# A decoder block on one core: transposes, products and casts placed by hand between the output and the up projection, and a ninth warm-up matmul

## The chip, the cores and the metric

The kernel runs on one core of one Trainium2 chip. The metric is the device time of one execution in microseconds (us), given as the median of several runs. Engines are named as the profile names them: PE (TensorE matmuls), PEld (its weight loads), DVE (VectorE), ACT (ScalarE), POOL (GpSimd), SP (SyncE, here only a DMA queue).

## The reference

One layer, 512 tokens, width 1024, all in float32: attention and pooling are merged through gates, then comes the output projection, an MLP with a squared ReLU, and a last norm.

```python
h = rmsnorm(x, norm_attn_g[l])
u = h @ w_in[l]
u_q, u_k, u_v, u_pool, u_gate = jnp.split(u, splits, axis=-1)
...
a = diff_attention(q, k, v, positions, lam, subln_g[l], lam_init)
p = multiscale_pool(u_pool, w_pool[l], pool_scale[l])
gates = jax.nn.sigmoid(u_gate.reshape(B, S, N_BRANCHES, D_MODEL))
merged = gates[:, :, 0] * a + gates[:, :, 1] * p
x = x + (merged @ w_out[l]).astype(x.dtype)
h2 = rmsnorm(x, norm_mlp_g[l])
z = jnp.square(jax.nn.relu(h2 @ w_up[l]))
x = x + (z @ w_down[l]).astype(x.dtype)
...
return rmsnorm(x, final_norm_g)
```

`w_out` is 1024x1024, `w_up` 1024x4096, `w_down` 4096x1024.

## The kernel before

Every float32 product is made of three matmuls in a rounded format: each operand is split into a high part (`wh`, `hi`, a cast on ACT) and a remainder (`wl`, `lo`, a subtraction on DVE), and high by high, remainder by high and high by remainder are summed in PSUM. So each block of weights costs a DMA, a cast and a remainder before PE may use it. Before the first real matmul stand warm-up matmuls on a tile of ones (`warm`).

The change lies in the passage from the output projection to the MLP.

- The output projection runs over two halves n of its 1024 columns, with `w_out` in blocks of two k-tiles (`wr_o`, `wh_o`, `wl_o`). For n=0 four banks (`po`, one for each group of 128 tokens, t=0 to 3) grow together. For n=1 each t has a bank of its own (`po` rows 0 to 3, 24 matmuls each, through `mm_rows`). `x1_add` adds a bank to the residual `x1` (DVE) and squares the sum (ACT, `square`), from which `row_scale` makes the norm's factor; `h2` (`h` in the profile) is the normed row (DVE).
- Eight transposes on PE for each t turn `h2` into two banks (`h2T`, b=0 and 1). t=0 and t=2 share two banks, t=1 and t=3 another two. From the banks come the operands of the MLP: `gab` (high part on ACT, remainder on DVE), plain copies `h2f` (t=0, 1) and `hw` (t=2, 3) on ACT, and from these by sums and differences the forms S1 to S4 in `gss` (`forms_h2`).
- The MLP runs in four quarters q of its 4096 inner columns. In each, `up(q)` makes seven products A11, A12, A22, S1, S2, S3, S4 of 2x2 blocks in place of eight (a Strassen-like scheme) and `down(q)` seven more. One up product is 48 matmuls of 256 columns in two halves i, each in its own bank (`um_0`, `um_1`); one down product is 24 matmuls of 512 columns (`dm`). For q=0 the order of the up products is A11, A12, S1, S2, S3, A22, S4.
- S2, S3 and A22 add onto the banks of A11. After each, the bank is read: `keep` copies it to `rawz` (ACT), `join` adds it to `rawz` (DVE), `z_of` applies ReLU and square (ACT). The next product may add onto a half only when that half was read.
- The weights of S1, S2 and A22 are sums that stand in one pair of buffers (`wga`): when DVE has read one form, a DMA with addition on POOL's queue makes the next. Those of A11, A12, S4 come by SP (`wr_u`), those of S3 are `wal`. For the down weights of A11 and S1, DVE makes the sum `wga_d` of `wr_d` and `wal_d`.

A planner sets the order on each engine from its own estimate of times; every engine then runs its list strictly in that order and waits on semaphores. `after(later, earlier)` gives the planner a rule of order between two instructions. Two of the existing ones are touched by the change, one in `up(q)` and one at its end:

```python
if q == 0 and form == A11 and i + p == 2 and k == 0:
    after(m, state["h2T"])
```

The first down product, A11 of `down(0)`, needs `z` of A11 and its weights, and no later up product; nothing but the planner holds it.

Of the kernel before, what the change touches and what calls it, by code (L numbers as in the profile page):

```python
# [21 lines left out]
NK = D // P  # L22
# [29 lines left out]
def block_kernel(ctx, tc, xT, x_tok, gains, pos, consts, w_in, w_v, w_pool, w_out, w_up, w_dn, out):  # L52
# [113 lines left out]
        compare_op=ALU.is_ge, fill=NEG, base=0, channel_multiplier=1,  # L166
    )
    warm = bank(7, "warm")
    for _ in range(8):
        T.matmul(warm[:, :P], lhsT=ones, rhs=ones, start=True, stop=True)  # L170


# [386 lines left out]

    def square(t, n, junk):  # L560

        A.activation(out=junk, in_=x1[:, t, n * 512 : n * 512 + 512], func=AF.Square, accum_out=st[:, t, n : n + 1])

    def row_early(t, n):

# [13 lines left out]
    def mm_rows(a_, t, k, w, start, stop):  # L579
        hi, lo = w  # L580
        sl, tsl = slice((k % 2) * 512, (k % 2) * 512 + 512), slice(t * P, t * P + P)
        T.matmul(a_, lhsT=mh[:, k, tsl], rhs=hi[:, sl], start=start, stop=False)
        T.matmul(a_, lhsT=mh[:, k, tsl], rhs=lo[:, sl], start=False, stop=False)
        T.matmul(a_, lhsT=ml[:, k, tsl], rhs=hi[:, sl], start=False, stop=stop)

    def x1_add(t, n, a_):
        xs = x1[:, t, n * 512 : n * 512 + 512]
        V.tensor_tensor(out=xs, in0=a_, in1=xs, op=ALU.add)
        square(t, n, R[t][:, 0:2, :].rearrange("p a t -> p (a t)"))

    def forms_h2(forms, x):

# [18 lines left out]
                mm_rows(po[t], t, k, w, k == 0, k == NK - 1)  # L611
    for t in range(NT):
        nc.sync.dma_start(out=x1[:, t, :], in_=x_tok[t])
    for t in range(NT):
        x1_add(t, 0, po[t])
        row_early(t, 0)
    g2b, _ = gain(R[4].rearrange("p b c -> p (b c)"), 0)
    ws = [get_w(w_out[1, kk], f"o1_{kk}", V) for kk in range(4)]
    for t in range(NT):
        a_ = bank(4 + t, f"po1_{t}")  # L620
        for k in range(NK):
            mm_rows(a_, t, k, ws[k // 2], k == 0, k == NK - 1)
        x1_add(t, 1, a_)
        V.scalar_tensor_tensor(out=h2[:, t % 2], in0=x1[:, t, :], scalar=row_scale(t, 1), in1=g2b, op0=ALU.mult, op1=ALU.mult)
        pv = []
        for b in range(2):
            pt = bank((t % 2) * 2 + b, f"h2T{t}_{b}")
            for j in range(4):
                k = 4 * b + j
                state["h2T"] = T.transpose(out=pt[:, j * P : j * P + P], in_=h2[:, t % 2, k * P : k * P + P], identity=ident)  # L630
            pv.append(pt.rearrange("p (j q) -> p j q", q=P))
        sl = slice((t % 2) * P, (t % 2) * P + P)
        if t > 1:

            A.copy(out=hw[:, 1, :, sl], in_=pv[0])
            V.tensor_tensor(out=hw[:, 0, :, sl], in0=pv[1], in1=hw[:, 1, :, sl], op=ALU.subtract)
            forms_h2((S1, S2), sl)
        if t == 3:
            forms_h2((S3,), slice(0, HS))
        for b in range(t // 2, 2):  # L640
            hi, lo = (gab[b][:, t // 2, i, :, sl] for i in range(2))
            A.copy(out=hi, in_=pv[b])
            part = V.tensor_tensor(out=lo, in0=pv[b], in1=f(hi), op=ALU.subtract)
            if t == 3:
                after(part, state[S3])
            if t < 2:
                A.copy(out=h2f[:, b, :, sl], in_=pv[b])
# [8 lines left out]
    def weights(src, q, nm, order):  # L656

        def raw(b, tag="wr", pool=wp):
            if b == 2:
                both = big.tile([P, 2, 1024], F32, tag="s1b", name=f"wr21_{nm}{q}")  # L660
                tiles = [both[:, c] for c in range(2)]
            else:
                tiles = [pool.tile([P, 1024], F32, tag=tag, name=f"{tag}_{nm}{b}_{q}_{c}", bufs=2) for c in range(2)]
            if b is not None:
                for c in range(2):
                    nc.sync.dma_start(out=tiles[c], in_=src[q, b, c])
            return tiles

        def plus(tiles, b):

            return [G.dma_start(out=tiles[c], in_=src[q, b, c], accum_op=ALU.add) for c in range(2)]  # L671

        def parts(rs, b, hold=None, add=None):

            third = nparts[0] % 3 == 2
            nparts[0] += 1
            out_ = []
            for c in range(2):
                hi, lo = (
                    (bk if third else wp).tile([P, 1024], F32R, tag=t_ + "b" * third, name=f"{t_}_{nm}{b}_{q}_{c}", bufs=2 if third else 4)  # L680
                    for t_ in ("wh", "wl")
                )
                if add is None:
                    cast = split_w(rs[c], hi, lo, eng=V)
                else:

                    cast = A.copy(out=hi, in_=rs[c])
                    A.mul(out=lo, in_=f(hi), mul=-1.0)
                    G.dma_start(out=lo, in_=src[q, add, c], accum_op=ALU.add)
                if hold:  # L690
                    after(cast, hold)
                out_.append((hi, lo))
            return out_

        early = nm == "u" and q == 0
        r11, al, ga = raw(0), raw(1, "wal", bk), raw(None, "wga", bk)
        for c in range(2):
            if early:
                nc.sync.dma_start(out=ga[c], in_=src[q, 0, c])
            else:  # L700
                V.tensor_tensor(out=ga[c], in0=r11[c], in1=al[c], op=ALU.add)
        if early:
            plus(ga, 1)
            plus(al, 3)
        for n, form in enumerate(order):
            if form == A11:
                yield parts(r11, "b11", zhi[q, S1] if nm == "d" and q else None)
            elif form == A12:
                yield parts(raw(2), "b21", zhi[q, A11] if nm == "d" and q else None)
            elif form == S4:  # L710
                yield parts(raw(3), "b22", None, 3 if nm == "d" and q == 3 else None)
            elif form == S3:
                yield parts(al, "t3", first[-1])
            else:
                w = parts(ga, f"t{form}", state["rows"] if form == S1 and early else None if form == S1 else first[-1])
                if form != A22:
                    adds = plus(ga, {S1: 3, S2: 2}[form])
                if form == S1 and not early:

                    for i in plus(al, 3):  # L720
                        after(i, adds[1])
                yield w
# [23 lines left out]
    def up(q):  # L746
# [3 lines left out]
        def product(form, name, onto=None):  # L750
            w, pa = next(W), onto or [acc(f"u{name}{q}_{i}") for i in range(2)]
            rh, rl = gf[form]
            first.append(None)
            for i in range(2):
                hi, lo = w[i]
                for p in range(2):
                    a_ = pa[i][:, p * HS : p * HS + HS]
                    for k in range(4):
                        c = slice((p * 4 + k) * P, (p * 4 + k) * P + P)
                        m = T.matmul(a_, lhsT=hi[:, c], rhs=rh[:, k, :], start=p + k == 0 and onto is None, stop=False, skip_group_check=True)  # L760
                        first[-1] = first[-1] or m
                        T.matmul(a_, lhsT=hi[:, c], rhs=rl[:, k, :], start=False, stop=False, skip_group_check=True)  # L762
                    for k in range(4):
                        c = slice((p * 4 + k) * P, (p * 4 + k) * P + P)
                        m = T.matmul(a_, lhsT=lo[:, c], rhs=rh[:, k, :], start=False, stop=k == 3, skip_group_check=True)  # L765
                        if q == 0 and form == A11 and i + p == 2 and k == 0:
                            after(m, state["h2T"])

            if form == A22:
                state["m4"] = m  # L770
            elif form == S4:
                after(first[-1], state["m4"])
            return pa

        def keep(pa, r):
            for a_, r_ in zip(bank_view(pa), halves(r)):
                A.copy(out=r_, in_=a_)  # L777

        def join(pa, r):
            for a_, r_ in zip(bank_view(pa), halves(r)):  # L780
                V.tensor_tensor(out=r_, in0=a_, in1=r_, op=ALU.add)

        def z_of(r, sign, pa=None):
            for i, r_ in enumerate(halves(r)):
# [7 lines left out]
            forms_h2((S4,), slice(0, HS))  # L792

        def first_block():
            join(product(A12, "m2"), R[0])
            z_of(R[0], 1.0)
            if q > 0:
                zsplit(q, A11, R[0])
# [30 lines left out]
    def down(q):  # L829
# [15 lines left out]
        def product(form, name, onto=None):  # L845
            w, pa = next(W), onto or [acc(f"d{name}{q}_{a}") for a in range(2)]
            first.append(None)
            for a in range(2):
                m, _ = mms(pa[a], form, w, a, (0, 512), onto is None or onto is m2 and q == 0)
                first[-1] = first[-1] or m  # L850
            return pa

        def to_x1(pa, r, n):
# [140 lines left out]
```

## Time and profile before

| | |
|---|---|
| median of three runs | 677.72 us (676.64 to 678.88) |
| profiled execution | 675.88 us, span 674.1 us |
| mean granted PE clock over the span | 0.997 |
| output projection, n=1 row 3, to the first up matmul | 341 to 348.9 us |
| up products of q=0 | 348.9 to 394.9 us |
| costliest lines of PE | the three matmuls of `down`, L839, L841, L842: 7 to 8% of the chain each; the three of `up`, L760, L762, L765: 7% each |

Times within the execution are counted from the start of the span. The other 1.78 us of the execution lie around the span. A row of a timeline gives start, length, engine, line, operation, tile written and tiles read, shape, how many equal instructions it merges, and in brackets the idle time of the engine before it with what ended it. A matmul's length is modelled, so the distance from start to start tells its cost.

### The profile page before, as it was taken

Reading aid. Unit: us, or ns where it says so; the run is one execution under the profiler, and the core shown is the slowest. Engines: PE = TensorE matmul, PEld = TensorE weight load, DVE = VectorE, ACT = ScalarE, POOL = GpSimd, SP = SyncE. Lnnn points to the kernel's source line nnn. Section 1 sums busy time; section 2 is a strip of 40 time slices with the busy share of each in tenths; the row PEclk is TensorE's granted clock in tenths of the full one; section 3 lists DMA queues with packets and bytes.
Section 4 is the critical chain, followed back from the end, with each engine's and each line's share of the span. In section 5 each row is a group of like instructions: output and inputs, shape, how many; then the busy total and the mean of one; then the engine's idle time right before and its main releaser. Section 6 shows DMA issues by size and latency. Waiting matters only on the chain.

```text
span 674.1 us, 9988 instructions
## 1 busy us (share of the span) xinstructions
PE 664.5 (99%) x3686; PEld 579.4 (86%) x3686; DVE 526.4 (78%) x882; ACT 461.9 (69%) x741; POOL 112.0 (17%) x130
## 2 busy tenths in 40 slices
PE   9999999999999999999999999999999999999995
PEld 7888888888888888888889988899889998899884
DVE  5955977799979986965478989657994599747995
ACT  7465577978887698883477976367743696356974
POOL 2001110142133212520202020202103021210120
PEclk9999999999999999999999999999999999999998
DMA  8516464435254364574964688775959579494863
GB/s 304 174 60 182 124 150 127 101 95 124 94 133 122 98 159 95 128 197 172 314 186 84 198 176 231 159 204 138 237 187 192 194 155 261 123 215 129 215 125 124
DMA packets 32880, 109.34 MB, mean 162 GB/s; under 512 B 4032, under 2 KB 4928, under 8 KB 32832
## 3 DMA queue, kind: packets, MB, share of 16 engines
q0 software_dynamic: 10656, 38.80, 32.1%
q1 hardware_dynamic: 21744, 69.38, 28.8%
q8 instruction: 29, 0.48, 0.3%
q10 hardware_dynamic: 432, 0.52, 0.2%
q14 instruction: 19, 0.16, 0.1%
HBM read 106.59 MB, written 2.10 MB: 161 GB/s over the span
## 4 chain that ended last, share of the span: by engine, by line
PE 89%; DMA 5%; issue 3%; ACT 2%; DVE 1%; SPq 0%; POOLq 0%
PE dm L839 8%; PE dm L841 7%; PE dm L842 7%; PE um L760 7%; PE um L765 7%; PE um L762 7%; DMA wga_uNone<-w_up 4%; PE v L235 2%; PE o L418 2%; PE ga L132 2%; PE ga L131 2%; PE k L132 2%; PE gp L135 2%; PE gp L132 2%; PE k L131 2%
## 5 line engine op out<-in xcount | busy, mean ns | idle before, releaser
L841 PE MATMUL dm<-wh_dt,z 128*128 128x512 f32 (+1 forms) x128 | 49.5, 387 | 0.0
L842 PE MATMUL dm<-wl_dt,z 128*128 128x512 f32 (+1 forms) x128 | 49.4, 386 | 0.0
L839 PE MATMUL dm<-wh_dt,z 128*128 128x512 f32 (+1 forms) x128 | 49.0, 387 | 0.0
L760 PE MATMUL um<-gss,wh_ut 128*128 128x256 f32 x192 | 48.1, 284 | 0.1
L762 PE MATMUL um<-gss,wh_ut 128*128 128x256 f32 x192 | 48.1, 283 | 0.0
L401 ACT ACTIVATE p<-p,st 128x128 f32<-128x128 f32 (+3 forms) x64 | 35.7, 558 | 14.1 <-DVE st L397 13.8
L857 DVE TENSOR_TENSOR x<-x,dm 128x512 f32<-128x512 f32 x48 | 32.6, 683 | 15.2 <-PE dm L842 15.0
L112 ACT CAST wh_ut<-wga_uNone 128x1024 fp32r<-128x1024 f32 x24 | 24.9, 1052 | 27.5 <-PE dm L841 19.5
L671 POOL DMA_DIRECT2D wga_dNone<-w_dn x16 | 14.2, 885 | 150.9 <-DVE wl_dt L113 150.9
L112 ACT CAST wh_ub<-wr_u 128x1024 fp32r<-128x1024 f32 x24 | 25.1, 1048 | 20.0 <-PE um L762 11.0
L113 DVE TENSOR_TENSOR wl_ut<-wga_uNone,wh_ut 128x1024 fp32r<-128x1024 f32 x24 | 29.0, 1223 | 11.4 <-ACT wh_ut L112 10.2
L842 PE MATMUL dm<-wl_db,z 128*128 128x512 f32 x96 | 37.2, 389 | 0.0
L841 PE MATMUL dm<-wh_db,z 128*128 128x512 f32 x96 | 37.2, 389 | 0.0
L760 PEld LDWEIGHTS um<-gss,wh_ut 128*128 128x128 f32 x192 | 36.8, 192 | 0.3 <-ACT rawz L777 0.3
L762 PEld LDWEIGHTS um<-gss,wh_ut 128*128 128x128 f32 x192 | 36.9, 192 | 0.0
L839 PE MATMUL dm<-wh_db,z 128*128 128x512 f32 x96 | 35.8, 390 | 0.0
L671 POOL DMA_DIRECT2D wga_uNone<-w_up x18 | 15.6, 865 | 121.6 <-DVE wl_ut L113 87.5
L113 DVE TENSOR_TENSOR wl_ub<-wr_u,wh_ub 128x1024 fp32r<-128x1024 f32 x24 | 29.1, 1220 | 8.1 <-ACT wh_ub L112 8.1
L112 ACT CAST wh_dt<-wga_dNone 128x1024 fp32r<-128x1024 f32 x24 | 24.9, 1049 | 14.6 <-issue 5.0
L736 DVE TENSOR_TENSOR z<-rawz,z 128x1024 fp32r<-128x1024 f32 x28 | 33.7, 1221 | 0.5 <-ACT z L733 0.5
L397 DVE CUSTOM_DVE_ANT_0 p<-s,mask 128x128 f32<-128x128 f32 (+3 forms) x64 | 30.3, 484 | 3.6 <-PE s L396 3.5
L113 DVE TENSOR_TENSOR wl_dt<-wga_dNone,wh_dt 128x1024 fp32r<-128x1024 f32 x24 | 29.1, 1221 | 4.5 <-ACT wh_dt L112 4.5
(324 smaller groups left out, 2206.4 us busy)
## 6 DMA issues: line engine op xcount, KB each, us to landing
wr_u<-w_up SPq DMA_DIRECT2D x24, 512.0 KB, 5.3
wr_d<-w_dn SPq DMA_DIRECT2D x24, 512.0 KB, 4.0
wga_uNone<-w_up POOLq DMA_DIRECT2D x18, 512.0 KB, 6.8
wga_dNone<-w_dn POOLq DMA_DIRECT2D x16, 512.0 KB, 5.5
wr_k<-w_in SPq DMA_DIRECT2D x8, 512.0 KB, 3.3
wr_ga<-w_in SPq DMA_DIRECT2D x8, 512.0 KB, 3.3
wr_gp<-w_in SPq DMA_DIRECT2D x8, 512.0 KB, 3.8
wl_ga<-w_in POOLq DMA_DIRECT2D x8, 512.0 KB, 5.5
```

The costliest lines, as they stand in the source:

```text
L112: ins = A.copy(out=hi[:, sl], in_=raw[:, sl])
L113: (eng or G).tensor_tensor(out=lo[:, sl], in0=raw[:, sl], in1=f(hi)[:, sl], op=ALU.subtract)
L132: T.matmul(acc, lhsT=hi[:, c], rhs=rl[k], start=False, stop=False)
L401: A.activation(out=pr[:, c, :N], in_=pr[:, c, :N], func=AF.Exp, scale=-1.0, bias=st[:, c : c + 1], accum_out=st[:, 2 + c : 3 + c])
L736: V.tensor_tensor(out=z[:, 1], in0=r, in1=f(z[:, 0]), op=ALU.subtract)
L760: m = T.matmul(a_, lhsT=hi[:, c], rhs=rh[:, k, :], start=p + k == 0 and onto is None, stop=False, skip_group_check=True)
L762: T.matmul(a_, lhsT=hi[:, c], rhs=rl[:, k, :], start=False, stop=False, skip_group_check=True)
L765: m = T.matmul(a_, lhsT=lo[:, c], rhs=rh[:, k, :], start=False, stop=k == 3, skip_group_check=True)
L839: m = T.matmul(a_, lhsT=zh, rhs=hi[:, sl], start=p == 0 and start, stop=False, skip_group_check=True)
L841: T.matmul(a_, lhsT=zl, rhs=hi[:, sl], start=False, stop=False, skip_group_check=True)
L842: end = T.matmul(a_, lhsT=zh, rhs=lo[:, sl], start=False, stop=p == 3, skip_group_check=True)
L857: V.tensor_tensor(out=xs, in0=xs, in1=pa[a], op=(ALU.add, ALU.subtract)[n])
```

## The change

No arithmetic changes and no byte more is moved, but for one more warm-up matmul. The rest is rules of order: the transposes of t=0 and t=1 come inside `po` row 3, those of t=2 and t=3 inside A11 and A12; the matmuls of the up products of q=0 follow each other half by half (`state["um"]`); the first down product follows the last up product; the cast of the last `w_out` block precedes the first squares; A12's joins follow the remainder of S2's form; and the casts of A22's weights follow the copy of S2 (`state["keep"]`).

```diff
-    for _ in range(8):
+    for _ in range(9):
         T.matmul(warm[:, :P], lhsT=ones, rhs=ones, start=True, stop=True)
...
+    sq0 = []
     for t in range(NT):
-        x1_add(t, 0, po[t])
+        sq0.append(x1_add(t, 0, po[t]))
         row_early(t, 0)
     g2b, _ = gain(R[4].rearrange("p b c -> p (b c)"), 0)
-    ws = [get_w(w_out[1, kk], f"o1_{kk}", V) for kk in range(4)]
+    ws = []
+    for kk in range(4):
+        raw, hi, lo = load_w(w_out[1, kk], f"o1_{kk}")
+        cast = split_w(raw, hi, lo, eng=V)
+        ws.append((hi, lo))
+    for ins in sq0:
+        after(ins, cast)
     for t in range(NT):
         a_ = bank(4 + t, f"po1_{t}")
         for k in range(NK):
-            mm_rows(a_, t, k, ws[k // 2], k == 0, k == NK - 1)
+            m, end = mm_rows(a_, t, k, ws[k // 2], k == 0, k == NK - 1)
+            if t > 1 and k == 0:
+                after(m, state["po"])
+        if 0 < t < 3:
+            for b in range(2):
+                after(state["h2T", t - 1, b], end)
+        state["po"] = end
...
+                if j == 1:
+                    state["h2T", t, b] = state["h2T"]
                 state["h2T"] = T.transpose(out=pt[:, j * P : j * P + P], in_=h2[:, t % 2, k * P : k * P + P], identity=ident)
...
+                if early and b == f"t{A22}":
+                    after(cast, state["keep"])
...
-                        if q == 0 and form == A11 and i + p == 2 and k == 0:
+                        if q == 0 and form == A12 and (i, p, k) == (1, 0, 0):
                             after(m, state["h2T"])
+                    if q == 0:
+                        if (form, i, p) == (A11, 0, 1):
+                            for b in range(2):
+                                after(state["h2T", 2, b], m)
+                        elif (form, i, p) == (A11, 1, 1):
+                            for b in range(2):
+                                after(state["h2T", 3, b], m)
+                        if form != A11 or i + p:
+                            after(begin, state["um"])
+                        state["um"] = m
...
-            join(product(A12, "m2"), R[0])
+            join(product(A12, "m2"), R[0], None if q else state[S2])
...
+            if q == 0 and form == A11:
+                after(first[-1], state["um"])
```

How the rules move instructions, at the places of which the prediction speaks.

PE, from the end of `po` row 3 to the first up matmuls, before (`h2T_0`, `h2T_1` are the two banks of one t; the first two groups of eight are t=0 and t=1, the last group begins t=2):

```order
L630 MATMUL h2T_0_3200<-ident,h_2987 128x128 [waits DVE_49]
L630 MATMUL h2T_0_3200<-ident,h_2987 128x128 x3
L630 MATMUL h2T_1_3205<-ident,h_2987 128x128 x4
L630 MATMUL h2T_0_3249<-ident,h_2987 128x128 [waits DVE_49]
L630 MATMUL h2T_0_3249<-ident,h_2987 128x128 x3
L630 MATMUL h2T_1_3254<-ident,h_2987 128x128 x4
L583 MATMUL po_3_3317<-wl_o_3_3164,vh 128x512
L584 MATMUL po_3_3317<-wh_o_3_3163,vl 128x512
L760 MATMUL um_0_3398<-gab_2989,wh_ub_0_0_3390 128x256 [waits Activation_49]
L760 MATMUL um_1_3399<-gab_2989,wh_ub_0_1_3394 128x256
L760 MATMUL um_0_3464<-gab_2990,wh_ub_0_0_3456 128x256 [waits Activation_49]
L630 MATMUL h2T_0_3298<-ident,h_2987 128x128 [waits Activation_49]
```

The same place now, from the middle of `po` row 3:

```order
L645 MATMUL h2T_0_3201<-ident,h_2988 128x128 [waits DVE_49]
L645 MATMUL h2T_0_3201<-ident,h_2988 128x128 x3
L645 MATMUL h2T_1_3206<-ident,h_2988 128x128 x4
L582 MATMUL po_3_3318<-wh_o_2_3158,vh 128x512
L583 MATMUL po_3_3318<-wl_o_2_3159,vh 128x512
L584 MATMUL po_3_3318<-wh_o_2_3158,vl 128x512
L582 MATMUL po_3_3318<-wh_o_2_3158,vh 128x512
L583 MATMUL po_3_3318<-wl_o_2_3159,vh 128x512
L645 MATMUL h2T_0_3250<-ident,h_2988 128x128 [waits DVE_49]
L645 MATMUL h2T_0_3250<-ident,h_2988 128x128 x3
L645 MATMUL h2T_1_3255<-ident,h_2988 128x128 x4
L584 MATMUL po_3_3318<-wh_o_2_3158,vl 128x512
```

t=0's transposes moved from behind the 22nd matmul of row 3 to behind its 12th, t=1's to behind its 17th. The transposes of t=2, which began behind three up matmuls, now stand near the end of A11:

```order
L778 MATMUL um_1_3400<-gab_2990,wh_ub_0_1_3395 128x256
L781 MATMUL um_1_3400<-gab_2990,wh_ub_0_1_3395 128x256
L645 MATMUL h2T_0_3299<-ident,h_2988 128x128 [waits DVE_49,PE_49,Activation_49]
L645 MATMUL h2T_0_3299<-ident,h_2988 128x128 x3
L645 MATMUL h2T_1_3304<-ident,h_2988 128x128 [waits PE_49,Activation_49]
L645 MATMUL h2T_1_3304<-ident,h_2988 128x128 x3
L784 MATMUL um_1_3400<-gab_2990,wl_ub_0_1_3396 128x256 x4
L778 MATMUL um_0_3465<-gab_2991,wh_ub_0_0_3457 128x256
```

All eight of t=2 stand in one piece ahead of A11's last four matmuls, and A12 (`um_0_3465`) follows.

ACT, around the copies of S2 out of its banks (`COPY rawz<-um_0_3398` and `um_1_3399`; the `wh_ub` casts are weights of S4, the `wh_ut` casts those of A22, `gss` is the S4 form), before:

```order
L777 COPY rawz<-um_1_3531 128x512 [waits PE_49]
L112 CAST wh_ub_0_0_3775<-wr_u_0_0_3771 128x1024 [waits DMAHW7_49,PE_49]
L777 COPY rawz<-um_0_3398 128x512 [waits PE_49]
L112 CAST wh_ut_0_0_3704<-wga_uNone_0_3382 128x1024 [waits DMASW4_49]
L112 CAST wh_ut_0_1_3708<-wga_uNone_1_3383 128x1024 [waits DMASW5_49]
L112 CAST wh_ub_0_1_3779<-wr_u_0_1_3772 128x1024 [waits DMAHW0_49,DVE_49,PE_49]
L603 CAST gss_2992<-hw 128x1024 [waits DVE_49]
L777 COPY rawz<-um_1_3399 128x512 [waits PE_49]
```

and now (`um_0_3399` and `um_1_3400` are the same banks):

```order
L112 CAST wh_ub_0_0_3776<-wr_u_0_0_3772 128x1024 [waits DMAHW7_49,PE_49]
L817 ACTIVATE rawz<-rawz 128x512 [waits Activation_49]
L806 COPY rawz<-um_0_3399 128x512 [waits PE_49]
L112 CAST wh_ub_0_1_3780<-wr_u_0_1_3773 128x1024 [waits DMAHW0_49,PE_49]
L806 COPY rawz<-um_1_3400 128x512 [waits PE_49]
L603 CAST gss_2993<-hw 128x1024 [waits DVE_49]
L112 CAST wh_ut_0_0_3705<-wga_uNone_0_3383 128x1024 [waits DMASW4_49]
L112 CAST wh_ut_0_1_3709<-wga_uNone_1_3384 128x1024 [waits DMASW5_49]
```

The copy of S2's second half moved ahead of the S4 form and of both casts of A22's weights.

DVE, around the joins of S3 (`rawz<-um`, first and second half), from the remainder of S4's first weights, before:

```order
L113 TENSOR_TENSOR wl_ub_0_0_3776<-wr_u_0_0_3771,wh_ub_0_0_3775 128x1024 [waits DMAHW7_49,PE_49,Activation_49]
L113 TENSOR_TENSOR wl_ut_0_0_3705<-wga_uNone_0_3382,wh_ut_0_0_3704 128x1024 [waits DMASW4_49,Activation_49]
L113 TENSOR_TENSOR wl_ut_0_1_3709<-wga_uNone_1_3383,wh_ut_0_1_3708 128x1024 [waits DMASW5_49,Activation_49]
L113 TENSOR_TENSOR wl_ub_0_1_3780<-wr_u_0_1_3772,wh_ub_0_1_3779 128x1024 [waits DMAHW0_49,PE_49,Activation_49]
L781 TENSOR_TENSOR rawz<-um_0_3398,rawz 128x512 [waits PE_49]
L604 TENSOR_TENSOR gss_2992<-hw,gss_2992 128x1024 [waits Activation_49]
L701 TENSOR_TENSOR wga_dNone_0_3863<-wr_d_0_0_3855,wal_d_0_0_3859 128x1024 [waits DMAHW5_49,DMAHW3_49,DVE_49]
L736 TENSOR_TENSOR z_0_3760<-rawz,z_0_3760 128x1024 [waits Activation_49]
L113 TENSOR_TENSOR wl_db_0_0_3868<-wr_d_0_0_3855,wh_db_0_0_3867 128x1024 [waits Activation_49]
L781 TENSOR_TENSOR rawz<-um_1_3399,rawz 128x512 [waits PE_49]
```

and now:

```order
L113 TENSOR_TENSOR wl_ub_0_0_3777<-wr_u_0_0_3772,wh_ub_0_0_3776 128x1024 [waits DMAHW7_49,PE_49,Activation_49]
L113 TENSOR_TENSOR wl_ub_0_1_3781<-wr_u_0_1_3773,wh_ub_0_1_3780 128x1024 [waits DMAHW0_49,PE_49,Activation_49]
L604 TENSOR_TENSOR gss_2993<-hw,gss_2993 128x1024 [waits Activation_49]
L810 TENSOR_TENSOR rawz<-um_0_3399,rawz 128x512 [waits PE_49]
L113 TENSOR_TENSOR wl_ut_0_0_3706<-wga_uNone_0_3383,wh_ut_0_0_3705 128x1024 [waits DMASW4_49,Activation_49]
L113 TENSOR_TENSOR wl_ut_0_1_3710<-wga_uNone_1_3384,wh_ut_0_1_3709 128x1024 [waits DMASW5_49,Activation_49]
L753 TENSOR_TENSOR z_0_3761<-rawz,z_0_3761 128x1024 [waits Activation_49]
L718 TENSOR_TENSOR wga_dNone_0_3864<-wr_d_0_0_3856,wal_d_0_0_3860 128x1024 [waits DMAHW5_49,DMAHW3_49,DVE_49]
L810 TENSOR_TENSOR rawz<-um_1_3400,rawz 128x512 [waits PE_49]
```

The remainder of S4's second weights moved ahead of the joins, A22's remainders between them, and `wl_db` out from between them; the sum `wga_dNone_0` still stands ahead of the second join.

More of the change, by code (lines that the diff above doesn't have):

```diff
@@ L560, in square @@
     def square(t, n, junk):
-        A.activation(out=junk, in_=x1[:, t, n * 512 : n * 512 + 512], func=AF.Square, accum_out=st[:, t, n : n + 1])
+        return A.activation(out=junk, in_=x1[:, t, n * 512 : n * 512 + 512], func=AF.Square, accum_out=st[:, t, n : n + 1])
     def row_early(t, n):
@@ L581, in mm_rows @@
         sl, tsl = slice((k % 2) * 512, (k % 2) * 512 + 512), slice(t * P, t * P + P)
-        T.matmul(a_, lhsT=mh[:, k, tsl], rhs=hi[:, sl], start=start, stop=False)
+        m = T.matmul(a_, lhsT=mh[:, k, tsl], rhs=hi[:, sl], start=start, stop=False)
         T.matmul(a_, lhsT=mh[:, k, tsl], rhs=lo[:, sl], start=False, stop=False)
-        T.matmul(a_, lhsT=ml[:, k, tsl], rhs=hi[:, sl], start=False, stop=stop)
+        return m, T.matmul(a_, lhsT=ml[:, k, tsl], rhs=hi[:, sl], start=False, stop=stop)
     def x1_add(t, n, a_):
@@ L588, in x1_add @@
         V.tensor_tensor(out=xs, in0=a_, in1=xs, op=ALU.add)
-        square(t, n, R[t][:, 0:2, :].rearrange("p a t -> p (a t)"))
+        return square(t, n, R[t][:, 0:2, :].rearrange("p a t -> p (a t)"))
     def forms_h2(forms, x):
@@ L756, in product @@
                 for p in range(2):
+                    begin = None
                     a_ = pa[i][:, p * HS : p * HS + HS]
@@ L761, in product @@
                         first[-1] = first[-1] or m
+                        begin = begin or m
                         T.matmul(a_, lhsT=hi[:, c], rhs=rl[:, k, :], start=False, stop=False, skip_group_check=True)
@@ L776, in keep, with join @@
             for a_, r_ in zip(bank_view(pa), halves(r)):
-                A.copy(out=r_, in_=a_)
-        def join(pa, r):
+                state["keep"] = A.copy(out=r_, in_=a_)
+        def join(pa, r, hold=None):
             for a_, r_ in zip(bank_view(pa), halves(r)):
-                V.tensor_tensor(out=r_, in0=a_, in1=r_, op=ALU.add)
+                ins = V.tensor_tensor(out=r_, in0=a_, in1=r_, op=ALU.add)
+                if hold:
+                    after(ins, hold)
         def z_of(r, sign, pa=None):
```

## The prediction

> **What bounds the kernel now.** I read the page's busy shares and chain first, then the waits of TensorE (PE) over the whole span, then the timeline of PE from 318 to 400 us, where the change lies, then ACT, DVE, POOL and SP in the same stretch.
>
> ```profile
> PE 664.5 (99%) x3686; PEld 579.4 (86%) x3686; DVE 526.4 (78%) x882; ACT 461.9 (69%) x741; POOL 112.0 (17%) x130
> PE 89%; DMA 5%; issue 3%; ACT 2%; DVE 1%; SPq 0%; POOLq 0%
> ...
> PE warm L170 <- POOL eps L161: 1.1, 1, 1.1
> PE h2T L630 <- ACT h2f L647: 0.6, 1, 0.6
> PE v L235 <- ACT wh_v L112: 0.3, 1, 0.3
> PE um L760 <- ACT gss L603: 0.2, 1, 0.2
> ```
>
> PE is busy 99% and carries 89% of the chain; the waits view (us in all, times, longest) names only four pauses, two of them in the passage (`h2T`, `um`). A matmul's recorded length is modelled and longer than its turn, so the waits view understates a pause. I therefore count starts: work is the number of matmuls times their spacing, and what is left over is lost.
>
> ```profile
> 346.39 0.39 PE L582 MATMUL po<-wh_o,vh 128*128 128x512 f32 x1
> 346.62 1.91 PE L630 MATMUL h2T<-ident,h 128*128 128x128 f32 x16
> 348.29 0.48 PE L583 MATMUL po<-wl_o,vh 128*128 128x512 f32 x1
> 348.60 0.40 PE L584 MATMUL po<-wh_o,vl 128*128 128x512 f32 x1
> 348.88 0.87 PE L760 MATMUL um<-gab,wh_ub 128*128 128x256 f32 x3
> 350.36 0.66 PE L630 MATMUL h2T<-ident,h 128*128 128x128 f32 x4 [0.61 <-ACT h2f L647]
> ...
> 363.43 0.40 PE L760 MATMUL um<-gss,wh_ut 128*128 128x256 f32 x2
> 364.51 0.64 PE L765 MATMUL um<-gss,wl_ut 128*128 128x256 f32 x4
> 365.95 0.64 PE L765 MATMUL um<-gss,wl_ut 128*128 128x256 f32 x4
> 377.35 0.64 PE L765 MATMUL um<-gss,wl_ut 128*128 128x256 f32 x4
> 378.16 0.38 PE L760 MATMUL um<-gss,wh_ub 128*128 128x256 f32 x1 [0.17 <-ACT gss L603]
> 378.64 0.39 PE L760 MATMUL um<-gss,wh_ut 128*128 128x256 f32 x1
> 378.86 0.28 PE L762 MATMUL um<-gss,wh_ut 128*128 128x256 f32 x1
> ```
>
> Spacings: a 512-column `po` matmul 0.23 (346.39 to 346.62); 16 transposes from 346.62 to 348.29, 0.104 us each; twelve 256-column matmuls from 364.51 to 365.95, 0.120 each. The first `po` matmul behind transposes took 0.31 (348.29 to 348.60), 0.08 more than the usual. An up product is 48 matmuls, 5.76 us.
>
> First loss: from 348.88 to 363.43 stand two products (A11, A12: 11.52) and the 16 transposes of t=2 and t=3 (1.67), 13.19 of work in 14.55: 1.36 lost. Second loss: the row at 377.35 ends its four turns at 377.83. One matmul of S4 then waits, and the second half of S3 starts at 378.64, its second matmul 0.10 late at 378.86: 0.91 gone for one matmul of 0.12, 0.79 lost. Together 2.15 us, 0.32% of the execution, is all that this stretch holds. What held PE:
>
> ```profile
> 326.92 0.63 ACT L562 ACTIVATE rawz<-x 128x512 f32<-128x512 f32 x1 [1.20 <-DVE x L588]
> 347.26 2.05 ACT L642 CAST gab<-h2T 128x512 fp32r<-128x512 f32 x4 [0.86 <-PE h2T L630]
> 349.72 1.73 ACT L647 COPY h2f<-h2T 128x512 f32<-128x512 f32 x3 [0.41 <-DVE gab L643]
> 374.10 2.11 ACT L112 CAST wh_ut<-wga_uNone 128x1024 fp32r<-128x1024 f32 x2
> 376.12 1.04 ACT L112 CAST wh_ub<-wr_u 128x1024 fp32r<-128x1024 f32 x1
> 377.06 1.05 ACT L603 CAST gss<-hw 128x1024 fp32r<-128x1024 f32 x1
> 378.01 0.57 ACT L777 COPY rawz<-um 128x512 f32<-128x512 f32 x1
> ...
> 348.95 1.88 DVE L643 TENSOR_TENSOR gab<-h2T,gab 128x512 fp32r<-128x512 f32 x3
> ```
>
> First loss: the transposes of t=0 and t=1 come as one block just ahead of A11, so ACT's casts (347.26) and DVE's remainders (348.95) come as PE already needs them, and t=2's transposes stop behind the `h2f` copies that free their bank. Second: the copy that must read S2's second half before S3 adds onto it is queued behind four casts and the S4 form, and starts at 378.01, though S2 ended at 374.95 (363.43 plus 11.52).
>
> **The change part by part.**
>
> *Transposes of t=0, t=1 into `po` row 3; A11 in a row.* No matmul is added. Row 3 starts 22 matmuls of 0.23 ahead of 346.62, at 341.6; t=0's transposes now stand behind its 12th (344.3), t=1's behind its 17th (346.4). A11 still starts at 348.88, but with the casts of t=0 done. The last operand is t=1's remainder: ACT's second A12 weight cast waits for row 3's 12th matmul and ends near 345.9, DVE's remainder of it near 347.1 (1.13), three `gab` remainders of 0.60 (the 1.88 row) end near 348.9, when PE's second matmul wants one. I charge 0.1; ends 0 and 0.6 (one more `gab` remainder).
>
> *t=2 and t=3 later, inside A11 and A12.* t=2's transposes now follow 44 matmuls, at 354.2; `h` of t=2 needs only DVE's add of row 3 (about 349.7), two short steps and 1.28, near 351.7; the four `h2f` copies end near 350.4. t=3's stand near 356.2, its `h` near 353.6. So nothing waits, 2.5 us of cover each. Two returns from transposes to matmuls remain, 0.08 each as behind 348.29. S1 could start at 348.88 + 13.19 + 0.16 = 362.2 instead of 363.43: **-1.2**. The row-3 block is now two: **+0.1** for one more return.
>
> *What S1 and S2 then need.* S2's weights are added by POOL once DVE has read S1's:
>
> ```profile
> 357.40 2.35 DVE L113 TENSOR_TENSOR wl_ut<-wga_uNone,wh_ut 128x1024 fp32r<-128x1024 f32 x2
> 358.91 0.86 POOL L671 DMA_DIRECT2D wga_uNone<-w_up  x1 [26.05 <-DVE wl_ut L113]
> 366.88 1.06 ACT L112 CAST wh_ut<-wga_uNone 128x1024 fp32r<-128x1024 f32 x1 [0.37 <-DMA wga_uNone<-w_up]
> ```
>
> DVE now reads them behind `h` of t=3, from about 353.6, so POOL's queue moves some 4 us ahead. S2 would start near 368.2: even if these loads came no earlier, the cast for its second half would end at 367.9, before that half's 371. Cost 0. SP's and POOL's own orders are unchanged.
>
> *Casts of A22's weights behind S2's copy.* The copy follows S2's end (now near 373.9) by some 0.2, takes 0.57 and ends 2 us before S3's second half: **-0.8**. Queued behind it on ACT are S4's form and A22's two casts, 1.05 each, done by 377.9; A22 starts near 379.7: covered.
>
> *A new wait.* With S4 moved behind A22, A22 follows S3 directly and adds onto the banks that DVE's join of S3 reads. The join of the second half now stands behind DVE's sum of down weights.
>
> ```profile
> 376.34 2.35 DVE L113 TENSOR_TENSOR wl_ut<-wga_uNone,wh_ut 128x1024 fp32r<-128x1024 f32 x2
> 378.62 1.22 DVE L113 TENSOR_TENSOR wl_ub<-wr_u,wh_ub 128x1024 fp32r<-128x1024 f32 x1
> 379.75 0.69 DVE L781 TENSOR_TENSOR rawz<-um,rawz 128x512 f32<-128x512 f32 x1
> 380.35 1.22 DVE L604 TENSOR_TENSOR gss<-hw,gss 128x1024 fp32r<-128x1024 f32 x1
> ```
>
> By these starts a join takes 0.60, a 1024-wide step 1.13. From the end of S3's first half DVE owes: join 0.60, A22's two weight remainders 2.28, z's remainder 1.13, the sum 1.13, the second join 0.69: 5.83, plus about 0.2 for PE's result to be seen. PE arrives after 5.76. Wait 0.3 and 0.10 for restarting (as at 378.86): **+0.4**. Ends: 0 (the 5.83 absorbed by earlier DVE slack) and 1.5 (one more 1.13 step ahead).
>
> *First down product behind the last up product.* Eight `dm` matmuls ran between the products; now all follow. The work is the same, and z and its weights are ready near 386, PE there near 391.6: 0.
>
> *Cast of the last output weight ahead of the squares; A12's joins behind S2's form.* The cast (1.05) falls mostly into the 1.20 that ACT sat idle before its first square at 326.92, and the squares' next readers come 10 us later. A12's joins move from 361 to 367, where DVE has S2's remainders done, and their reader is a `relu` of R[0], wanted for z only near 378: 0 for both. If ACT's gap were closed, the squares would shift by at most 1.05, still far from row 3.
>
> *Ninth warm-up.*
>
> ```profile
> 1.14 3.78 PE L170 MATMUL warm<-onesr 128*128 128x128 f32 x16 [1.14 <-POOL eps L161]
> 5.24 1.19 PE L235 MATMUL v<-wh_v,xh 128*128 128x512 f32 x4 [0.32 <-ACT wh_v L112]
> 8.16 1.19 PE L235 MATMUL v<-wh_v,xh 128*128 128x512 f32 x4
> ```
>
> Eight warm-ups leave 16 records, 0.236 each against 0.104 for equal-sized transposes: they ran at half rate, while the first four products took the same 1.19 at 5.24 as at 8.16, full rate. The ninth adds two records, at most 0.47, into a 0.32 pause that ends with ACT's cast. I take 0, as eight already gave full rate; ends +0.15 (0.47 less 0.32) and, where full rate comes late, a gain (rival D). [...]
>
> Sum: 0.1 + 0.1 - 1.2 - 0.8 + 0.4 = **-1.4 us**. PE is the chain before and after the passage and nothing there is removed, so it reaches the end. Against the profiled execution: 675.88 (span 674.1 and 1.78 around it) becomes 674.5. That execution lies 1.84 below the median of the runs; applied to the median, 677.72 - 1.4 = **676.3**.
>
> **The rivals.**
> A. Both losses go and the new wait does not come, because DVE runs ahead: -1.9 to -2.1, 675.7. For it: DVE's 78% leaves slack. Against: its five steps start from PE's own half product. Chance 0.16.
> B. The new order makes other pauses as long as those removed, in the re-sorted ACT and DVE queues: 677.4 to 677.9. For it: two margins here are below 0.5. Against: the rest are 1 to 3 us. Chance 0.13.
> C. Slower. DVE's sum in front of the join also waits for the down weights' load:
>
> ```profile
> 376.46 11.74 SPq L666 DMA_DIRECT2D wr_d<-w_dn  x4
> 380.48 1.05 ACT L112 CAST wh_db<-wr_d 128x1024 fp32r<-128x1024 f32 x1 [0.94 <-DMA wr_d<-w_dn]
> ...
> wr_u<-w_up SPq DMA_DIRECT2D x24, 512.0 KB, 5.3
> ```
>
> Released near 374.3, it needed 4.0 (376.46 to 380.48) and has until 380.7, 6.4. From 6.4 on each us is PE's; from 7.8 the change loses, and at twice the median of 5.3 for such loads it costs 10.6 - 7.8 = 2.8: 680.5. Chance 0.04.
> D. In other executions full rate comes later than 5.24, and the ninth warm-up brings it forward: at most half of the 2.92 from 5.24 to 8.16, 1.5 more: 674.8. For it: the runs differ by 2.2. Against: eight sufficed in the one execution seen, and the pause filled is 0.32. Chance 0.06.
>
> **How the numbers follow.** The forecast, 0.7 to 1.9 us saved, has 0.61: 676.3, alone 675.6 to 677.2. The runs of before spread from 676.64 to 678.88, so a median is uncertain by some 0.6; with A, B and D the range is 674.7 to 678.0. About 0.3% (2.0 us) is what a measurement of this kernel can tell from no change. Faster by more: half of A, most of D, a sixth of the forecast and some scatter, 0.27; slower: C and a little of B, 0.06; within: 0.67.
>
> **What would show it.** In the changed profile: 32 transposes in four groups of eight, none with a wait on `h2f`; S1's first matmul 13.2 to 13.5 behind A11's; no pause between S3's halves; one pause of 0.2 to 0.6 at A22's second half, released by DVE's join; no down matmul before S4's end. I am wrong if A22's second half waits over 1 us, if a transposing group waits for `h`, or if the median moves by more than 2.5 us.

## The result and the profile after

The changed kernel takes 675.35 us (median of 22 runs, 674.47 to 676.38), the kernel before 676.13 (22 runs, 675.21 to 678.88). The ratio is 0.9983, with a 95% interval of 0.9976 to 0.9990: 1.15 us faster by it (0.7 to 1.6), 0.78 by the two medians. The three runs of before that were shown ahead of the prediction lay high.

The two profiled spans are nearly the same (674.1 and 674.0), so the gain is not read from them but from pieces of the two traces. I split each into the opening up to PE's 61st product on record (60 stand before it; the expectation of e8 calls it the 60th), the long stretch from there to A11's first matmul, and the passage with all that follows, from A11's first matmul to PE's last (starts, in us):

| piece | before | after | difference |
|---|---|---|---|
| PE's 61st product starts at | 19.19 | 19.96 | +0.77 |
| from there to A11's first matmul | 329.68 | 329.70 | +0.02 |
| A11's to S1's first matmul | 14.56 | 13.27 | -1.29 |
| pause between S3's halves | 0.79 | 0 | -0.79 |
| pause ahead of A22's second half, with its restart | 0 | 1.28 | +1.28 |
| A11's first to PE's last matmul | 317.78 | 316.86 | -0.92 |

The passage gained 0.92; the two losses and the new pause make 0.80 of it, and 0.12 more lies at the first down matmuls, of which eight stood among the up products before. Of this 0.06 is one longer spacing in the kernel before, at 398.96; what the rest hangs on was not followed up. The opening was 0.77 later in this one execution, for a reason that has nothing to do with the passage (below). PE in the changed kernel's timeline, in the columns of the prediction's rows (start, length, engine, line, operation, idle time before it and its releaser):

```profile
345.15 1.03 PE L645 MATMUL h2T<-ident,h 128*128 128x128 f32 x8
347.18 1.03 PE L645 MATMUL h2T<-ident,h 128*128 128x128 f32 x8
349.66 0.28 PE L778 MATMUL um<-gab,wh_ub 128*128 128x256 f32 x1
354.97 1.04 PE L645 MATMUL h2T<-ident,h 128*128 128x128 f32 x8
357.03 1.04 PE L645 MATMUL h2T<-ident,h 128*128 128x128 f32 x8
362.93 0.28 PE L778 MATMUL um<-gss,wh_ut 128*128 128x256 f32 x1
...
376.85 0.64 PE L784 MATMUL um<-gss,wl_ut 128*128 128x256 f32 x4
377.33 0.28 PE L778 MATMUL um<-gss,wh_ut 128*128 128x256 f32 x1
382.61 0.64 PE L784 MATMUL um<-gab,wl_ut 128*128 128x256 f32 x4
384.30 0.36 PE L778 MATMUL um<-gab,wh_ut 128*128 128x256 f32 x1 [1.05 <-DVE rawz L810]
393.00 0.40 PE L870 MATMUL dm<-wh_db,z 128*128 128x512 f32 x1
```

The four groups of eight transposes stand without a wait, S1 starts 13.27 behind A11, S3's second half follows its first after 0.48, which is its four turns of 0.12. Then the row at 382.61 ends its turns at 383.09, and A22's second half starts only at 384.30: 1.21 lost, and 0.07 more on the way back to full spacing. The row names DVE's join. DVE and ACT around it:

```profile
365.71 1.23 DVE L113 TENSOR_TENSOR wl_ut<-wga_uNone,wh_ut 128x1024 fp32r<-128x1024 f32 x1 [1.81 <-ACT wh_ut L112]
...
374.93 2.35 DVE L113 TENSOR_TENSOR wl_ub<-wr_u,wh_ub 128x1024 fp32r<-128x1024 f32 x2
377.20 1.22 DVE L604 TENSOR_TENSOR gss<-hw,gss 128x1024 fp32r<-128x1024 f32 x1
378.33 0.68 DVE L810 TENSOR_TENSOR rawz<-um,rawz 128x512 f32<-128x512 f32 x1
378.94 2.35 DVE L113 TENSOR_TENSOR wl_ut<-wga_uNone,wh_ut 128x1024 fp32r<-128x1024 f32 x2
381.20 1.22 DVE L753 TENSOR_TENSOR z<-rawz,z 128x1024 fp32r<-128x1024 f32 x1
382.34 1.22 DVE L718 TENSOR_TENSOR wga_dNone<-wr_d,wal_d 128x1024 f32<-128x1024 f32 x1
383.47 0.68 DVE L810 TENSOR_TENSOR rawz<-um,rawz 128x512 f32<-128x512 f32 x1
...
364.63 1.05 ACT L112 CAST wh_ut<-wga_uNone 128x1024 fp32r<-128x1024 f32 x1 [2.08 <-DMA wga_uNone<-w_up]
...
375.12 0.58 ACT L806 COPY rawz<-um 128x512 f32<-128x512 f32 x1
376.55 2.00 ACT L112 CAST wh_ut<-wga_uNone 128x1024 fp32r<-128x1024 f32 x2
```

ACT's copy now starts at 375.12, 2.2 ahead of S3's second half, with the casts behind it. DVE has no idle time in brackets from 374.93 to the join: S3's first half ended at 377.33, but its join waits until 378.33 behind S4's remainder (L604), and the second join stands behind two more steps.

### The profile page after: what moved, and what is told of

Read it like the earlier page. It is cut to its first block, busy times and chain, and to the rows that moved or that the text cites. A ratio compares the mean times of both kernels' runs of the same rounds, so it can differ in the third digit from the quotient of the medians.

```text
span 674.0 us, 9993 instructions
## 1 busy us (share of the span) xinstructions
PE 664.3 (99%) x3688; PEld 580.4 (86%) x3688; DVE 526.4 (78%) x882; ACT 461.3 (68%) x741; POOL 112.2 (17%) x130
## 4 chain that ended last, share of the span: by engine, by line
PE 96%; DVE 2%; DMA 1%; issue 0%; ACT 0%; SPq 0%; DVEq 0%
PE um L778 8%; PE um L781 8%; PE dm L870 7%; PE dm L872 7%; PE um L784 7%; PE dm L873 7%; PE v L235 2%; PE o L418 2%; PE ga L132 2%; PE ga L131 2%; PE gp L135 2%; PE gp L132 2%; PE k L132 2%; PE k L131 2%; PE gp L131 2%; PE k L135 2%
## 5 line engine op out<-in xcount | busy, mean ns | idle before, releaser
L686 POOL DMA_DIRECT2D wga_dNone<-w_dn x16 | 14.2, 887 | 154.9 <-DVE wl_dt L113 154.9
L750 ACT CAST z<-rawz 128x1024 fp32r<-128x1024 f32 x28 | 28.5, 1046 | 6.5 <-PE dm L873 2.8
```

## The experiments

Every kernel was compared with the kernel before on the same chip. The table gives the ratio, and from each profile the same pieces as above (us). Where a pause has a number, restarting costs 0.07 to 0.1 more.

| run | ratio (95%) | 61st product | A11 to S1 | pause S3 | pause A22 | A11 to last |
|---|---|---|---|---|---|---|
| changed kernel | 0.9983 (0.9976-0.9990) | 19.96 | 13.27 | 0 | 1.21 | 316.86 |
| e1 both steps behind the join | 0.9957 (0.9942-0.9972) | 19.09 | 13.27 | 0 | 0 | 315.59 |
| e2 casts behind the copy alone | 0.9987 (0.9975-1.0000) | 19.13 | 14.61 | 0 | 0 | 316.92 |
| e3 no placing | 1.0044 (1.0028-1.0059) | 19.35 | 17.29 | 0 | 0.71 | 320.39 |
| e4 eight warm-ups | 0.9987 (0.9974-1.0000) | 19.98 | 13.28 | 0 | 1.07 | 316.73 |
| e5 A22 and S4 interleaved | 0.9972 (0.9962-0.9983) | 19.41 | 13.27 | 0 | 0 | 315.59 |
| e6 no row 3 rule | 1.0010 (1.0000-1.0020) | 19.55 | 14.58 | 0 | 1.43 | 318.40 |
| e7 no rule on t=2, t=3 | 0.9988 (0.9979-0.9998) | 19.00 | 13.29 | 0 | 1.06 | 316.73 |
| e8 no warm-ups | 1.0014 (1.0002-1.0025) | 22.46 | 13.29 | 0 | 0.71 | 316.37 |
| e9 the sum behind the join | 0.9961 (0.9948-0.9974) | 19.66 | 13.28 | 0 | 0.05 | 315.71 |
| e10 first down product free | 0.9983 (0.9971-0.9994) | 19.26 | 13.27 | 0 | 0.95, ahead of two down matmuls | 316.73 |

**e1: what holds A22's second half.**

```
+                if nm == "d" and q == 0:
+                    after(ins, state["s3"])
...
+        if q == 0 and form == A11:
+            after(rem, state["s3"])
```

`ins` is the sum of down weights, `rem` z's remainder, and `state["s3"]` S3's second join.

> The changed kernel, with DVE's two steps of 1.13 us (z's remainder and the sum of down weights) ordered behind S3's second join. My theory: PE's pause of 1.21 us ahead of A22's second half comes from DVE's queue alone, so it falls to 0 to 0.15 us, nothing else gets slower, and the time falls by a further 1.1 to 1.3 us against the changed kernel: ratio to the kernel before 0.996 to 0.9975. Rival: the two steps that are put off are late for their own readers, and a pause of about 1 us comes between A22 and the first down products: ratio 0.998 to 0.9985, as the changed kernel.

674.01 us, 1.34 below the changed kernel's median and 1.27 less from A11 to the last matmul; the ratio is a little better than expected. DVE, then PE:

```profile
378.07 2.35 DVE L113 TENSOR_TENSOR wl_ut<-wga_uNone,wh_ut 128x1024 fp32r<-128x1024 f32 x2
380.34 0.68 DVE L814 TENSOR_TENSOR rawz<-um,rawz 128x512 f32<-128x512 f32 x1
380.94 1.21 DVE L755 TENSOR_TENSOR z<-rawz,z 128x1024 fp32r<-128x1024 f32 x1
382.07 1.21 DVE L718 TENSOR_TENSOR wga_dNone<-wr_d,wal_d 128x1024 f32<-128x1024 f32 x1
...
381.72 0.64 PE L788 MATMUL um<-gab,wl_ut 128*128 128x256 f32 x4
382.20 0.28 PE L782 MATMUL um<-gab,wh_ut 128*128 128x256 f32 x1
```

The join is done near 381.0 and PE goes from half to half in 0.48. The rival falls: no pause came elsewhere. This version beats both kernels, and with no pause left in the passage it is as short as the matmuls and returns there allow.

**e9: the same with one step.** Only the first of the two rules, that on the sum.

> The changed kernel with only the sum of down weights put behind S3's second join on DVE; z's remainder stays ahead of it. My theory: the pause at A22's second half is the length of DVE's queue less PE's half product, so taking one step of 1.13 us out of it shortens the pause from 1.06 to 1.21 us (as in the runs with this queue) to 0 to 0.15, as far as putting off both steps did: ratio 0.996 to 0.9978. Rival: the sum waited for its load and the rest of the queue is not full, so the pause shrinks by less, to 0.4 us or more: ratio 0.9978 to 0.9985.

```profile
382.00 0.69 DVE L812 TENSOR_TENSOR rawz<-um,rawz 128x512 f32<-128x512 f32 x1
...
382.30 0.64 PE L786 MATMUL um<-gab,wl_ut 128*128 128x256 f32 x4
382.83 0.35 PE L780 MATMUL um<-gab,wh_ut 128*128 128x256 f32 x1
```

The half starts 0.53 behind instead of 0.48. One step of 1.13 out of the queue took some 1.16 off the pause (1.21 to 0.05): the pause is DVE's queue, step by step, and the sum did not wait for its load.

**e5: cover instead of a shorter queue.** PE may put S4 between A22's halves again:

```
-    if form != A11 or i + p:
+    if form not in (A22, S4) and (form != A11 or i + p):
```

> The changed kernel without the strict order on A22 and S4: PE then takes half of S4's product between S3 and A22's first half and the other S4 half between A22's halves, while DVE's order up to S3's second join stays as in the changed kernel. My theory: the new pause comes from A22's second half standing too close behind S3's second half, so with other work between them the late join (about 383.5) is covered, PE's pause falls to 0 to 0.15 us and the time to that of the run in which the join was moved forward: ratio 0.996 to 0.9975. Rival: S4's half comes too early for its own operands and PE waits there instead, 0.5 us or more: ratio 0.998 or above.

```profile
383.43 0.64 PE L784 MATMUL um<-gab,wl_ut 128*128 128x256 f32 x4
383.91 0.28 PE L778 MATMUL um<-gss,wh_ub 128*128 128x256 f32 x1
385.35 0.28 PE L778 MATMUL um<-gab,wh_ut 128*128 128x256 f32 x1
```

S4's matmuls stand from 383.91 to 385.35 and A22's second half starts without a wait; A11 to last is 315.59, exactly as in e1. So the pause came from the strict order of A22 behind S3 together with the late join; either can be mended.

**e2: the casts alone, on the kernel before.**

```
+                if early and b == f"t{A22}":
+                    after(cast, state["keep"])
...
+                state["keep"] = A.copy(out=r_, in_=a_)
```

> The kernel before, with one part of the change: A22's weight casts behind ACT's copy of S2. My theory: the pause between S3's halves (0.79 us) goes, the first loss stays (S1 about 14.5 us behind A11's start), and since S4's second half still stands between A22's two halves here, DVE's join of S3 has cover and no new pause comes: 0.7 to 0.9 us faster, ratio 0.9985 to 0.999. Rival: the casts behind the copy bring a new pause by themselves, at A22's weights or its second half, of 0.5 us or more: ratio 0.9993 to 1.0005.

```profile
350.36 0.66 PE L630 MATMUL h2T<-ident,h 128*128 128x128 f32 x4 [0.67 <-ACT h2f L647]
...
377.34 0.64 PE L767 MATMUL um<-gss,wl_ut 128*128 128x256 f32 x4
377.82 0.28 PE L762 MATMUL um<-gss,wh_ub 128*128 128x256 f32 x1
377.94 0.28 PE L762 MATMUL um<-gss,wh_ut 128*128 128x256 f32 x1
```

S4's one matmul and S3's second half follow at once: the second loss is gone (0.86 from A11 to last), the first is still there with its wait on `h2f`. S4 matmuls stand between A22's halves in this order, and nothing new appears.

**e6, e7, e3: which of the placing rules matters.** e6 drops the rules on row 3, e7 those on t=2 and t=3 (with t=3 held where it was before), e3 both (lines shortened):

```
e6, e3  -    if t > 1 and k == 0: after(m, state["po"])
        -    if 0 < t < 3: after(state["h2T", t - 1, b], end)
e7, e3  -    after(state["h2T", 2, b], m); after(state["h2T", 3, b], m)
```

> The changed kernel without the rule that puts the transposes of t=0 and t=1 into row 3 (they come 2 and 4 matmuls later, each); the rules on t=2 and t=3 stay. My theory: the first loss hung on the operands of t=1, so A11 waits at its start for DVE's remainder of t=1: S1 13.9 to 14.6 us behind A11's start instead of 13.27, ratio 0.9988 to 1.0002. Rival: only the place of t=2 and t=3 mattered: S1 13.2 to 13.5 us behind A11's start, ratio 0.998 to 0.9987.

> The changed kernel without the rules on t=2 and t=3: both groups stand together ahead of A11's last four matmuls, about 0.9 us earlier for t=3. My theory: h of t=3 is ready near 354.3 and the group stands near 355.8, so nothing waits and nothing is lost: S1 13.2 to 13.4 us behind A11's start, ratio 0.998 to 0.9987. Rival: as in the run without any placing, DVE's h of t=3 is late and PE stands: S1 15 us or more behind A11's start, ratio 1.001 or above.

> The changed kernel without the rules that place the transposes (the rules on t=0 and t=1 in row 3, and on t=2 and t=3 inside A11 and A12; t=3's are held at the old place); the products' strict order, the casts behind the copy and all else stay. My theory: the transposes' place is what the first loss hung on, so S1 starts 14.2 to 14.8 us behind A11's start instead of 13.27, and the time is 1.0 to 1.5 us above the changed kernel's: ratio 0.9998 to 1.0007. Rival: the strict order of the products alone removes the first loss: S1 13.2 to 13.6 us behind A11, ratio 0.998 to 0.9987.

e6, PE at A11's start and DVE's remainder; then e7, the group of 16; then e3, PE and DVE:

```profile
349.26 0.28 PE L773 MATMUL um<-gab,wh_ub 128*128 128x256 f32 x1
350.63 0.39 PE L776 MATMUL um<-gab,wh_ub 128*128 128x256 f32 x1 [1.10 <-DVE gab L653]
...
349.90 0.68 DVE L653 TENSOR_TENSOR gab<-h2T,gab 128x512 fp32r<-128x512 f32 x1
```

```profile
354.03 1.91 PE L645 MATMUL h2T<-ident,h 128*128 128x128 f32 x16
```

```profile
349.95 1.06 PE L640 MATMUL h2T<-ident,h 128*128 128x128 f32 x8 [0.60 <-DVE h L632]
359.23 1.06 PE L640 MATMUL h2T<-ident,h 128*128 128x128 f32 x8 [3.07 <-DVE h L632]
...
355.46 1.23 DVE L113 TENSOR_TENSOR wl_ut<-wga_uNone,wh_ut 128x1024 fp32r<-128x1024 f32 x1
356.67 1.22 DVE L113 TENSOR_TENSOR wl_ut<-wga_uNone,wh_ut 128x1024 fp32r<-128x1024 f32 x1
357.81 1.28 DVE L632 SCALAR_TENSOR_TENSOR h<-x,st,rawz 128x1024 f32<-128x1024 f32 x1
```

Without the row 3 rule A11's second matmul waits for the remainder of t=1: 14.58 from A11 to S1, as much as in the kernel before, but at another wait (there t=2's transposes waited for `h2f`), so the equal size says nothing of the cause. Without the rules on t=2 and t=3 the 16 transposes stand in a row with no wait: 13.29. So the 1.29 needs the row 3 rule, and the rules on t=2 and t=3 add nothing beside it; without it they matter, as 14.58 in e6 against 17.29 in e3 shows. Row 3's rule without the strict order was not run. e6's ratio lies above the 0.9988 to 1.0002 that were expected: its pause at A22 is 1.43, and the section after this one shows why. e3 is a miss. I expected 14.2 to 14.8 and it came to 17.29, slower than before: the strict order, kept without any placing, leaves PE nothing to do while the group of t=3 waits, and DVE computes h of t=3 behind S1's two weight remainders at 355.46 and 356.67. In the kernel before, A12's matmuls went ahead there. The strict order is a cost that only the placing pays for.

**e10: the first down product free.**

```
-    if q == 0 and form == A11:
-        after(first[-1], state["um"])
```

> The changed kernel without the rule that puts the first down product behind the last up product: two of its matmuls then stand between A22's halves. My theory: the rule is worth nothing but the cover of two matmuls; they need z's remainder, ready near 382.4, so they fill 0.46 us of the pause at A22's second half if they are ready, and the time is 0 to 0.5 us below the changed kernel's: ratio 0.9975 to 0.9987. Rival: their weights' remainder or z is late and PE waits there longer than for the join: ratio 0.999 to 1.001.

```profile
383.28 0.50 PE L870 MATMUL dm<-wh_db,z 128*128 128x512 f32 x1 [0.79 <-ACT rawz L816]
383.85 0.36 PE L778 MATMUL um<-gab,wh_ut 128*128 128x256 f32 x1
```

The two down matmuls did not fill the pause; they waited themselves until 383.28. The rule is worth nothing either way: from A11 to the last matmul it is 316.73 and 316.86, and e4 and e7 have 316.73 too.

**e4 and e8: the warm-ups.** `range(9)` becomes `range(8)` and `range(0)`.

> The changed kernel with eight warm-up matmuls, as before, instead of nine. My theory: the ninth is worth nothing, since the first value product waits for ACT's cast in any case: ratio 0.998 to 0.9987 as with nine, first value product within 0.1 us of the end of ACT's cast. Rival: the ninth brings full clock forward in part of the executions: then eight cost 0.3 to 1 us, ratio 0.9988 to 0.9998. A third: the ninth delays the first value product, and eight gain 0.15 us, which only the profile could show.

> The changed kernel with no warm-up matmuls at all. My theory: warm-ups bring forward the time of full rate, but one more of them does not: with none, the products run at half rate from about 5.3 until 8.5 to 12, so the 60th product starts at 20.8 to 22.8 instead of the 19.1 to 20.0 of all runs so far, and the time is 1.2 to 3.3 us above the changed kernel's: ratio 1.000 to 1.003. Rival: full rate comes at the same time of 5.8 to 7.5 whatever runs before it: ratio 0.998 to 0.9987, 60th product at 19 to 20.

The openings of the changed kernel, of e1 (also nine warm-ups) and of e8:

```profile
1.14 4.21 PE L170 MATMUL warm<-onesr 128*128 128x128 f32 x18 [1.14 <-POOL eps L161]
5.58 1.82 PE L235 MATMUL v<-wh_v,xh 128*128 128x512 f32 x4 [0.24 <-ACT wh_v L112]
```

```profile
1.14 3.72 PE L170 MATMUL warm<-onesr 128*128 128x128 f32 x18 [1.14 <-POOL eps L161]
5.33 1.20 PE L235 MATMUL v<-wh_v,xh 128*128 128x512 f32 x4 [0.47 <-ACT wh_v L112]
```

```profile
5.90 2.08 PE L235 MATMUL v<-wh_v,xh 128*128 128x512 f32 x4 [5.90 <-ACT wh_v L112]
```

The same 18 records take 4.21 in one execution and 3.72 in the other. In e1 their spacing falls from 0.213 to 0.111 at 4.2, in the changed kernel the products' falls from 0.43 to 0.23 only at 7.0, in e4 with eight at 7.2, and without warm-ups at 11.9. So warm-ups are worth some 2.1 us together (0.9983 to 1.0014), and full rate comes at a time that differs by 2.8 us between two equal openings with nine (4.2 and 7.0). The profiles show no effect of the ninth: eight gave full rate from the first products in the kernel before (0.23 apart from 5.57 on), nine did not in the changed kernel. The ratios of e4 and the changed kernel cannot exclude an effect of some 1 us. (e8's profile also records a granted clock of 0.948, all others 0.996 to 0.999; its matmuls do not show it, since its 316.37 is e1's 315.59 with the pause of 0.71 and 0.07 for restarting.)

## Why the prediction was right, and where it was not

The two old pauses went as forecast. The one new pause came where it was forecast, but three times as long, because DVE was still at earlier work when its part of the count began.

The predicted move was -1.4; measured were -1.15 by the ratio, -0.78 by the medians and -0.92 from A11 to the last matmul. The time, 675.35, lies in the range and 0.95 below the 676.3: the median of three runs that it started from was 1.6 above that of 22, and the saving was 0.6 less by the medians, so the two errors offset each other in part. All that the prediction named as its signs came but one: the pause at A22's second half was to be 0.2 to 0.6, and "I am wrong if A22's second half waits over 1 us" came true with 1.21. The new wait was 0.9 longer than forecast, and the other terms together came 0.4 better, so the sum is nearer to the measurement than its largest wrong term.

- *First loss, -1.2:* measured -1.29. S1 13.27 behind A11's start, within the 13.2 to 13.5 that were named. e6 and e7 add that it needs the row 3 rule and, beside it, none on t=2 and t=3.
- *Remainder of t=1 late, +0.1:* it was not; A11's second matmul came 0.11 behind its first.
- *One more return, +0.1:* 0.02 or nothing from the 61st product to A11.
- *Second loss, -0.8:* measured -0.79; e2, with this part alone, gains 0.86 from A11 to the last matmul.
- *S2's weights, first down product, cast and squares, A12's joins, ninth warm-up, 0 each:* PE waits for none of these behind the opening; e10 bears out the down product, the profiles of e4 the ninth warm-up. The cast and squares and A12's joins were not undone by themselves.
- *The new wait, +0.4:* this is the term that was mis-sized: 1.21, with restarting 1.28. Its place and its releaser were right, its end of 1.5 held, and "one more 1.13 step ahead" is nearly what happened. The step that failed is the count "from the end of S3's first half", as if DVE stood free there. It was 1.0 behind, with S4's remainder still in work from 377.20 to 378.33. The 5.83 themselves were right: from 378.33 they end at 384.16, and PE starts at 384.30.

Why DVE was behind goes back to the load of S2's weights, which I had put at 0 for PE's sake. The row at 365.71 waited for ACT's cast at 364.63, and that cast for the load; behind it DVE has no idle time up to the second join. In eight runs with the same DVE order up to the first join of S3 (e5, e7, e4, e9, the changed kernel, e1, e6, e10) this remainder starts 2.60, 2.63, 2.64, 2.75, 2.78, 2.81, 3.00 and 3.15 behind S1, and the join 12.62 behind it each time: what the load loses, the join loses. In the four of them in which nothing but that queue delays A22, the pause is 1.06 (e7), 1.07 (e4), 1.21 (the changed kernel) and 1.43 (e6), each 1.57 less than its remainder's start. So a load can cost PE nothing at its own reader and still set a wait 18 us later. In e8, where the remainder starts at 1.89, the join came 13.00 behind it, with 0.20 of idle time between, and the pause was 0.71. That the landing causes it is read from these rows; no run moved the load.

Rival A (no new wait, because DVE runs ahead) did not come: DVE ran behind. e1 and e5 take the wait away, by a rule more or a rule less. Rival B came in part: a new pause took back 1.28 of the 2.08 removed, but it is the one that the forecast names, and no other stands in the passage. Rival C did not come: DVE's sum started right behind z's remainder. Of rival D the condition is true, full rate does come later than 5.24 in other executions, but nine warm-ups did not keep it from coming at 7.0; the timing alone does not exclude the rival.

Counted from PE's first matmul, full rate came 3.1 us later in e1 and 5.9 in the changed kernel (nine warm-ups each), 6.1 in e4 (eight) and 6.0 in e8 (none, so from its first product). No run shows what sets this time.

## What to carry to other kernels

When an order is fixed by hand, count the queue of the engine that frees the next buffer from its last idle moment, not from the moment its input is ready; here the difference was 1.0 us, and the new wait's term was off by 0.9. Then move what has no near reader behind the step that PE waits for: two rules in e1 more than doubled the gain. Undo rules one at a time, since some (t=2 and t=3, the down product) did nothing beside the others, and together, since the strict order without any placing lost 2.6 us.

## What the hardware showed beside that

Two executions of the same opening differ by up to 0.96 us at the 61st product (19.00 in e7, 19.96 in the changed kernel), from the time at which full rate comes (4.3 and 7.0) and from the landing of the first weights (ACT's cast at 4.59 and 4.91). One profiled span per kernel can therefore hide a gain of 0.9 us, as it did here; the stretch from the 61st product to A11 repeats to 0.2 us, and A11 to S1 to 0.02 where its order is the same.
